# Memory output projection in one bank, token differences on DVE, weight stores on SP's queue

## The chip, the cores and the metric

One core of a Trainium2 chip runs the whole program in one launch. The metric is the device time of that launch in microseconds (us). TensorE (PE) does the matrix products; VectorE (DVE), ScalarE (ACT) and GpSimd (POOL) do element work; SyncE (SP) only issues DMA transfers, which ACT can issue too, each engine through a queue of its own.

## The reference, cut to what matters

One layer of a decoder on 2048 new prompt tokens and 32 sample tokens, width 1024, all in float32:

```python
def mem_attend(hn, mk, mv, wq_x, wo_x):
    q = (hn @ wq_x).reshape(B, T, MEM_HEADS, MEM_DH)
    s = jnp.einsum('bthd,bmhd->bhtm', q, mk) * (MEM_DH ** -0.5)
    p = jax.nn.softmax(s, axis=-1)
    o = jnp.einsum('bhtm,bmhd->bthd', p, mv).reshape(B, T, D_MODEL)
    return o @ wo_x

def conv_ffn(hn, buf, w_gate, w_up, conv_w, conv_b, w_down):
    g = hn @ w_gate
    gp = jnp.concatenate([buf, g], axis=1)
    c = conv_b + sum(conv_w[j] * gp[:, j:j + T] for j in range(CONV_W))
    return (jax.nn.gelu(c) * (hn @ w_up)) @ w_down, gp[:, -(CONV_W - 1):]

def layer(x, ...):
    m, S, sv = mixer(rmsnorm(x, g_mix), s0, mix_p)
    h = x + m
    h = h + mem_attend(rmsnorm(h, g_x), mk, mv, wq_x, wo_x)
    f, new_buf = conv_ffn(rmsnorm(h, g_ffn), buf, ...)
    return h + f, S, new_buf, sv
```

The FFN is 2816 wide, the memory has 256 tokens and 4 heads.

## The kernel before

The prompt runs in four blocks of 512 tokens; the sample tokens ride with block 1 in the mixer and with block 2 in the FFN, whose tiles are then 544 wide. Activations are kept transposed: h is eight tiles of 128 model rows by the block's tokens, and "m" numbers these tiles. Float32 accuracy comes from splitting every operand into a high part (ACT, L84) and a low part (DVE, L85); `mm3` (L91 to 94) then issues three matmuls for one product, high by high, high by low and low by high.

Each block goes through norm, input projection, gated linear attention and SGU, an output projection (tiles `wo`), memory attention, a memory output projection (tiles `wx`), and the FFN. Values and output weights of the memory are folded beforehand into `vod`, so the `wx` stage multiplies the softened and transposed probabilities (`pTh`, `pTl`, made by `turn` from p for each head, two k tiles a head) with `vod`. It is a product with 8 k tiles for each of the 8 m tiles. `out_proj_steps` writes it as steps `half(m2, k0, last)`: for the m tiles 2 m2 and 2 m2 + 1, four k tiles from k0 on, 12 matmuls of 512 columns into an accumulator bank, and a DVE add of the bank to h (L1167). The list x1 holds the four steps with k0 = 0, x2 those with k0 = 4. So every m tile takes two banks and two adds, and the m tiles are finished in x2, one after the other. In `finish(m)` ACT scales h (`wxg`, L1175) and squares it (`wxq`, L1187), and POOL sums the squares over m (`wxsq`, L1192).

Blocks 1 to 3 do the FFN's gate and up products with seven block products in place of eight (`seven_step`, gate rows `wg`, up rows `wup`). These need sums and differences of weights, and of tokens: `seven_tokens` takes two scaled m tiles and makes t13 on DVE (L188, L189), t24 on POOL (L190, L191), and the high and low parts of the four operands: `w` (A11), `wbh`/`wbl`, `wth`/`wtl` and `wuh`/`wul`. The first gate product of a block runs "early": it goes through the first three token pairs for all seven products (names such as `a_wg30A`, `a_wg30S`) and then takes the last pair, m = 6 and 7. Beside it `stat` multiplies the sum of squares with a column of ones (`wxss`, L1199), DVE makes `rt` (L300), POOL raises it to the power -1/2 (`wxrs`, L301), DVE writes it on a diagonal (`dg_f`, L308) and PE spreads it over partitions (`bcp_f`, L309).

Block 0 does its FFN with plain products from weights that it loads, 512 KB a unit, on SP's queue (L102). While they are here it also makes what blocks 1 to 3 will load: split weights (`wkeep` for the down projection, array wd) and, in `seven_make`, the plain parts (w7g, w7u) and the sums (s7g, s7u). Their stores, 2 for each down unit, 10 for a gate and 8 for an up unit, 440 in all, go through `put` and `flush` (L290 to 296): `put` lists a store, `flush` issues what is listed on ACT's queue, two steps later or when the next unit is made. The stores of the folded memory weights go the same way, earlier.

`run` makes weight units five ahead of the step that uses them. Pools set how far work runs ahead: 4 accumulator banks and 4 more banks in PSUM, 5 raw weight buffers, 5 each of high and low weights, 49 wide token tiles. The order on each engine is set by a scheduler of the tile framework from the program's order, the dependences and its own estimate of times. `weave` (near the end of the program) merges lists of steps: the scores of the four heads and x1 form one list, and the turns of the four heads are put in at places 1, 2, 3 and 5.

Of the kernel before, what the change touches and what calls it, by code (L numbers as in the profile page):

```python
# [37 lines left out]
def hymba_step_kernel(  # L38
# [9 lines left out]
    nc = tc.nc  # L48
# [80 lines left out]
    def wkeep(dst, *spec):  # L129

        def load():
            out = wunit(*spec)
            flush()
            for x, t in enumerate(out):
                put(dst[:, x], t.bitcast(F32))
            return out
        return load
# [16 lines left out]
    def seven_make(raw, hi, lo, plain, sums, u, name):  # L154
# [10 lines left out]
        ks = slice(2 * u, 2 * u + 2)  # L165
        flush()
        for x, t in enumerate((hi, lo)):
            t = t.bitcast(F32).rearrange("p (k two) m -> p two k m", two=2)
            for k in range(2):
                put(plain[:, k, x, ks], t[:, k, :, 0:128])  # L170
            put(plain[:, 2, x, ks], t[:, 1, :, 128:256])
        for i, t in enumerate((s13, s24)):
            d = sums[:, 2 * i:2 * i + 2]
            v = lambda t: t.rearrange("p (s k m) -> p s k m", s=2, k=2)
            if len(sums.shape) == 4:
                put(d[:, :, ks], v(t[:, :512]))
                continue
            sh, sl = U(f"sh{i}{name}", F32R), U(f"sl{i}{name}", F32R)
            split(sh[:, :512], sl[:, :512], t[:, :512])
            for x, o in enumerate((sh, sl)):  # L180
                put(d[:, :, x, ks], v(o[:, :512].bitcast(F32)))

    def seven_tokens(a, b, H, name):
# [5 lines left out]
        dve.tensor_tensor(t13[:, hi_], B22, B12, ALU.subtract)  # L189
        pool.tensor_tensor(t24[:, lo_], B22, t13[:, lo_], ALU.subtract)  # L190
        pool.tensor_tensor(t24[:, hi_], B21, t24[:, lo_], ALU.subtract)  # L191
        one = U(f"w1{name}", F32R)
# [950 lines left out]

    def out_proj_steps(B, unit, src, g, name, sample, first, finished, keep=None, seven=False):

# [5 lines left out]

        def half(m2, k0, last):
            def fn(wu):
                wh, wl = wu
                x = src()
                if m2 == 0 and last:
                    B.hn, B.sq = [], None
                for mm in range(2):
                    m = 2 * m2 + mm
                    ms = slice(mm * 128, (mm + 1) * 128)  # L1160
                    for ci, (c0, cw) in enumerate(chunks_of(sample)):
                        cs = slice(c0, c0 + cw)
                        ps = acc(f"a_{name}{s}{k0}{m}{ci}")
                        for k in range(4):
                            mm3(ps[:, :cw], wh[:, k, ms], wl[:, k, ms], x[k0 + k][0][:, cs], x[k0 + k][1][:, cs],
                                k == 0, k == 3)
                        dve.tensor_tensor(B.h[m][:, cs], ps[:, :cw], B.h[m][:, cs], ALU.add)  # L1167
                    if last:
                        finish(m)
# [34 lines left out]

        second = 4 - first
        return ([half(m2, first, False) for m2 in range(4)], [half(m2, second, True) for m2 in range(4)], Step(stat))


# [400 lines left out]
    for s, B in enumerate(blocks):  # L1609
# [5 lines left out]
        if B.mix_sample:  # L1615
            def keep():
                if not hasattr(smp, "x"):
# [7 lines left out]
        x1, x2, xstat = out_proj_steps(B, lambda k0, m2, s=s: wready(vod[m2][k0 // 4], f"wx{s}{k0}{m2}"),  # L1625
                                       lambda B=B: B.ao, "gffn", "wx", False, 0, B.ffn_sample, seven=s > 0)
        steps += w2 + [stat, scales]
        steps += weave(sc + x1, (turns[:1], 1, 1), (turns[1:2], 2, 2), (turns[2:3], 3, 3), (turns[3:], 5, 5))
        fin = final_steps(B)
# [48 lines left out]
```

## Time and profile before

| | us |
|---|---|
| median of three runs | 2936.9 |
| lowest, highest | 2928.57, 2940.09 |
| the profiled execution | 2934.86 |
| its span, first to last instruction | 2933.1 |
| TensorE busy in it | 2870.4 |
| VectorE busy | 1816.2 |
| ScalarE busy | 1048.8 |
| GpSimd busy | 697.4 |
| mean granted TensorE clock, as a share of full speed | 0.988 |

All rows of the trace come from the one profiled execution, whose time is its span and 1.8 us around it. Engines work beside each other, so busy times don't add up to the span. A waiting time says which instruction had to be done before the waiting one could start. The block ends that matter lie near 1176, 1888 and 2570 us (blocks 1, 2 and 3, from the memory output projection to the FFN), and block 0's FFN lies between 400 and 800 us.

### The profile page before, as it was taken

The numbers are of one execution on the slowest core, as the hardware profiler recorded it, in microseconds if no ns is written. First come the engines' busy times: TensorE is split into PE (matmuls) and PEld (weight loads), VectorE is DVE, ScalarE is ACT, GpSimd is POOL, SyncE is SP. The second block draws the span as 40 slices with busy tenths as digits, with TensorE's granted clock in tenths as the row PEclk, the third lists the DMA queues.
The fourth block names the chain that finished last, engine by engine and source line by source line (L and its number), as shares of the span: only waits on it lengthen the run. The fifth ranks groups of instructions, "written<-read, shape, count | busy, mean of one in ns | idle before, by whom it ended". The sixth has DMA issues, their size and how long they took to land.

```text
span 2933.1 us, 47340 instructions
## 1 busy us (share of the span) xinstructions
PE 2870.4 (98%) x18148; PEld 2533.2 (86%) x18148; DVE 1816.2 (62%) x3109; ACT 1048.8 (36%) x1904; POOL 697.4 (24%) x724
## 2 busy tenths in 40 slices
PE   8999999999999999999999999999999999999998
PEld 8887887887887898888888879899999788899998
DVE  6566567777746544645556674566666685475555
ACT  5635334333462423312223543422223534331222
POOL 1222112111122321312223231332222232141221
PEclk9999999999999999999999999999999999999999
DMA  9645679999832235776896214477776323567774
GB/s 309 198 144 184 204 231 324 344 343 337 301 104 64 67 115 184 277 277 246 306 327 232 84 58 151 167 254 262 252 266 223 105 67 106 182 245 253 281 278 179
DMA packets 360137, 625.48 MB, mean 213 GB/s; under 512 B 27195, under 2 KB 227838, under 8 KB 359912
## 3 DMA queue, kind: packets, MB, share of 16 engines
q1 hardware_dynamic: 232040, 513.37, 51.5%
q10 hardware_dynamic: 127872, 109.09, 11.0%
q8 instruction: 144, 2.36, 0.3%
q14 instruction: 81, 0.66, 0.1%
HBM read 497.04 MB, written 125.31 MB: 212 GB/s over the span
## 4 chain that ended last, share of the span: by engine, by line
PE 77%; DVE 6%; DMA 2%; ACT 2%; issue 1%; POOL 1%; ACTq 0%; DVEq 0%; POOLq 0%; SPq 0%
PE d L92 5%; PE d L94 5%; PE d L93 5%; PE sc L94 2%; PE sc L93 2%; PE sc L92 2%; PE a_wo L92 2%; PE a_wo L93 2%; PE a_wo L94 2%; PE a_wx L92 1%; PE a_wx L93 1%; PE a_wx L94 1%; PE a_wup L92 1%; PE a_wup L93 1%; PE a_wup L94 1%
## 5 line engine op out<-in xcount | busy, mean ns | idle before, releaser
L92 PE MATMUL d<-acth,whi_wd 128*128 128x512 f32 (+2 forms) x720 | 244.8, 340 | 0.0
L94 PE MATMUL d<-acth,wlo_wd 128*128 128x512 f32 (+2 forms) x720 | 243.2, 338 | 0.0
L93 PE MATMUL d<-actl,whi_wd 128*128 128x512 f32 (+2 forms) x720 | 242.7, 337 | 0.0
L1532 DVE TENSOR_TENSOR h<-d,h 128x512 f32<-128x512 f32 (+1 forms) x232 | 133.5, 583 | 159.4 <-PE d L94 159.2
L1471 POOL TENSOR_TENSOR c<-c,bc_f 128x512 f32<-128x512 f32 (+1 forms) x88 | 130.4, 1484 | 158.9 <-ACT c L1470 158.2
L94 PEld LDWEIGHTS d<-acth,wlo_wd 128*128 128x128 f32 x720 | 135.5, 188 | 16.0 <-issue 1.6
L92 PEld LDWEIGHTS d<-acth,whi_wd 128*128 128x128 f32 x720 | 135.5, 188 | 15.2 <-issue 1.6
L93 PEld LDWEIGHTS d<-actl,whi_wd 128*128 128x128 f32 x720 | 135.6, 188 | 14.4 <-issue 0.8
L94 PE MATMUL sc<-whi_qk,wol 128*128 128x256 f32 x512 | 144.5, 283 | 0.0
L92 PE MATMUL sc<-whi_qk,woh 128*128 128x256 f32 x512 | 144.3, 283 | 0.0
L93 PE MATMUL sc<-wlo_qk,woh 128*128 128x256 f32 x512 | 143.9, 282 | 0.0
L1461 ACT ACTIVATE c<-g,colsb 128x512 f32<-128x512 f32 x88 | 71.7, 814 | 200.8 <-DVE g L1430 142.6
L1493 POOL TENSOR_TENSOR c<-r_q_wup,c 128x512 f32<-128x512 f32 (+1 forms) x33 | 59.3, 1796 | 340.2 <-DVE r_q_wup L281 216.2
L1458 POOL COPY carry<-g 128x2 f32<-128x2 f32 x88 | 33.2, 377 | 423.1 <-DVE g L1430 421.0
L980 POOL TENSOR_TENSOR e<-e,k 128x512 f32<-128x512 f32 (+1 forms) x48 | 71.8, 1497 | 211.7 <-DVE kr L976 137.2
L92 PE MATMUL a_wo<-ch,h_wo 128*128 128x512 f32 (+1 forms) x320 | 113.2, 362 | 7.2 <-ACT ch L84 6.0
L93 PE MATMUL a_wo<-cl,h_wo 128*128 128x512 f32 (+1 forms) x320 | 113.9, 358 | 0.4 <-POOL cl L85 0.4
L94 PE MATMUL a_wo<-ch,l_wo 128*128 128x512 f32 (+1 forms) x320 | 113.3, 356 | 0.0
L1462 DVE SCALAR_TENSOR_TENSOR c<-g,colsb,c 128x512 f32<-128x512 f32 x88 | 86.9, 987 | 26.9 <-ACT c L1461 24.9
L92 PE MATMUL a_wx<-pTh,whi_wx 128*128 128x512 f32 x256 | 101.4, 396 | 0.0
L93 PE MATMUL a_wx<-pTl,whi_wx 128*128 128x512 f32 x256 | 100.6, 393 | 0.0
L94 PE MATMUL a_wx<-pTh,wlo_wx 128*128 128x512 f32 x256 | 100.6, 393 | 0.0
(3354 smaller groups left out, 9616.5 us busy)
## 6 DMA issues: line engine op xcount, KB each, us to landing
whi_wd<-wd SPq DMA_DIRECT2D x66, 512.0 KB
wlo_wd<-wd SPq DMA_DIRECT2D x66, 512.0 KB
r_wo<-in_w_out_dram SPq DMA_DIRECT2D x32, 512.0 KB
whi_qk<-qkd SPq DMA_DIRECT2D x32, 512.0 KB
wlo_qk<-qkd SPq DMA_DIRECT2D x32, 512.0 KB
wlo_wx<-vod SPq DMA_DIRECT2D x32, 512.0 KB
whi_wx<-vod SPq DMA_DIRECT2D x32, 512.0 KB
r_wg<-in_w_gate_dram SPq DMA_DIRECT2D x22, 512.0 KB
```

The source lines that it names most:

```text
L92: pe.matmul(ps, wh, xh, start=first, stop=False)
L93: pe.matmul(ps, wh, xl, start=False, stop=False)
L94: pe.matmul(ps, wl, xh, start=False, stop=last)
L980: pool.tensor_tensor(kl[:, :Tl], e[:, :Tl], B.k[p][:, :Tl], ALU.mult)
L1458: pool.tensor_copy(carry[:, f, :], g[:, SB:SB + 2])
L1461: act.activation(c[:, :SB], g[:, 2:SB + 2], AF.Identity, bias=cb, scale=w2)
L1462: dve.scalar_tensor_tensor(c[:, :SB], g[:, 1:SB + 1], w1, c[:, :SB], ALU.mult, ALU.add)
L1471: pool.tensor_tensor(c[:, :T], c[:, :T], B.fbc[:, :T], ALU.mult)
L1493: (dve, pool)[i].tensor_tensor(c[:, :T], q[i], c[:, :T], ALU.mult)
L1532: dve.tensor_tensor(B.h[m + mm][:, cs], ps[:, :cw], B.h[m + mm][:, cs], ALU.add)
```

## The change

It has three parts. (1) `out_proj_steps` gets a mode `whole`, used for `wx` in all four blocks. For m tiles 0 to 3 the first four k open a bank that stays open, in two steps, and two more steps close them; for m tiles 4 and 5, and then 6 and 7, a step with the first four k and a step with the last four follow each other. h is added once for each m tile, when its bank closes. The turn of head 3 moves from behind the second step of the stage to behind the first. (2) The two t24 differences move from POOL to DVE. (3) Block 0's 440 weight stores are issued on SP's queue, in the program right behind the unit that makes them, without the list. The stores of the folded memory weights stay on ACT.

```diff
         def load():
             out = wunit(*spec)
-            flush()
             for x, t in enumerate(out):
-                put(dst[:, x], t.bitcast(F32))
+                nc.sync.dma_start(dst[:, x], t.bitcast(F32))
...
-        flush()
         for x, t in enumerate((hi, lo)):
             t = t.bitcast(F32).rearrange("p (k two) m -> p two k m", two=2)
             for k in range(2):
-                put(plain[:, k, x, ks], t[:, k, :, 0:128])
-            put(plain[:, 2, x, ks], t[:, 1, :, 128:256])
+                nc.sync.dma_start(plain[:, k, x, ks], t[:, k, :, 0:128])
+            nc.sync.dma_start(plain[:, 2, x, ks], t[:, 1, :, 128:256])
...
-                put(d[:, :, ks], v(t[:, :512]))
+                nc.sync.dma_start(d[:, :, ks], v(t[:, :512]))
...
-                put(d[:, :, x, ks], v(o[:, :512].bitcast(F32)))
+                nc.sync.dma_start(d[:, :, x, ks], v(o[:, :512].bitcast(F32)))
...
-        pool.tensor_tensor(t24[:, lo_], B22, t13[:, lo_], ALU.subtract)
-        pool.tensor_tensor(t24[:, hi_], B21, t24[:, lo_], ALU.subtract)
+        dve.tensor_tensor(t24[:, lo_], B22, t13[:, lo_], ALU.subtract)
+        dve.tensor_tensor(t24[:, hi_], B21, t24[:, lo_], ALU.subtract)
...
-        def half(m2, k0, last):
+        open_ = {}
+
+        def half(m2, k0, last, begin=True, end=True):
...
-                        ps = acc(f"a_{name}{s}{k0}{m}{ci}")
+                        ps = acc(f"a_{name}{s}{k0}{m}{ci}") if begin else open_.pop(m)
                         for k in range(4):
                             mm3(ps[:, :cw], wh[:, k, ms], wl[:, k, ms], x[k0 + k][0][:, cs], x[k0 + k][1][:, cs],
-                                k == 0, k == 3)
-                        dve.tensor_tensor(B.h[m][:, cs], ps[:, :cw], B.h[m][:, cs], ALU.add)
+                                begin and k == 0, end and k == 3)
+                        if end:
+                            dve.tensor_tensor(B.h[m][:, cs], ps[:, :cw], B.h[m][:, cs], ALU.add)
+                        else:
+                            open_[m] = ps
...
         second = 4 - first
+        if whole:
+            out = [half(m2, first, False, end=False) for m2 in (0, 1)]
+            out += [half(m2, second, True, begin=False) for m2 in (0, 1)]
+            for m2 in (2, 3):
+                out += [half(m2, first, False, end=False), half(m2, second, True, begin=False)]
+            return out[:2], out[2:], Step(stat)
...
-        steps += weave(sc + x1, (turns[:1], 1, 1), (turns[1:2], 2, 2), (turns[2:3], 3, 3), (turns[3:], 5, 5))
+        steps += weave(sc + x1, (turns[:1], 1, 1), (turns[1:2], 2, 2), (turns[2:3], 3, 3), (turns[3:], 4, 4))
```

On DVE at the end of block 3's `wx` stage this stood before; h_6 and h_7 are the adds of the last two m tiles, `wtl_25663` and `wul_25667` belong to the pair before, `l_wup30S` is the low part of a weight.

```order
L1167 TENSOR_TENSOR h3_6_22821<-a_wx3460_25679,h3_6_22821 128x512
L85 TENSOR_TENSOR wtl35_25663<-t1335_25649,wth35_25662 128x512
L85 TENSOR_TENSOR wul35_25667<-t2435_25650,wuh35_25666 128x512
L1167 TENSOR_TENSOR h3_7_22822<-a_wx3470_25698,h3_7_22822 128x512
L85 TENSOR_TENSOR w137_25720<-wxg36_25693,w137_25720 128x256
L188 TENSOR_TENSOR t1337_25714<-wxg36_25693 128x256
L85 TENSOR_TENSOR l_wup30S2_25676<-r_wup30S2_25673,h_wup30S2_25675 128x1024
L189 TENSOR_TENSOR t1337_25714<-wxg37_25712,wxg36_25693 128x256
L85 TENSOR_TENSOR wbl37_25724<-wxg37_25712,wbh37_25723 128x512
L85 TENSOR_TENSOR wtl37_25728<-t1337_25714,wth37_25727 128x512
L85 TENSOR_TENSOR wul37_25732<-t2437_25715,wuh37_25731 128x512
```

And this stands there now:

```order
L1171 TENSOR_TENSOR h3_6_22773<-a_wx3060_25585,h3_6_22773 128x512
L85 TENSOR_TENSOR w137_25656<-wxg36_25630,w137_25656 128x256
L1171 TENSOR_TENSOR h3_7_22774<-a_wx3070_25598,h3_7_22774 128x512
L186 TENSOR_TENSOR t1337_25650<-wxg36_25630 128x256
L85 TENSOR_TENSOR l_wup30S2_25614<-r_wup30S2_25611,h_wup30S2_25613 128x1024
L187 TENSOR_TENSOR t1337_25650<-wxg37_25648,wxg36_25630 128x256
L188 TENSOR_TENSOR t2437_25651<-wxg37_25648,t1337_25650 128x256
L85 TENSOR_TENSOR wbl37_25660<-wxg37_25648,wbh37_25659 128x512
L189 TENSOR_TENSOR t2437_25651<-wxg37_25648,t2437_25651 128x256
L85 TENSOR_TENSOR wtl37_25664<-t1337_25650,wth37_25663 128x512
L85 TENSOR_TENSOR wul37_25668<-t2437_25651,wuh37_25667 128x512
```

One add for each tile is left, the pair before no longer stands between the last adds, and the two t24 differences (L188 and L189 of the new numbering) have come in ahead of `wbl` and ahead of `wtl`.

On PE at the same place, the end of the early part of the first gate product, before; `w_`, `wb`, `wt` and `wu` numbered 257xx are the operands of the last pair:

```order
L92 MATMUL a_wg30A12_25799<-wbh37_25723,wg30A12_25483 128x256
L93 MATMUL a_wg30A12_25799<-wbl37_25724,wg30A12_25483 128x256
L94 MATMUL a_wg30A12_25799<-wbh37_25723,wg30A12_25483 128x256
L92 MATMUL a_wg30S1_25789<-wth37_25727,wg30S1_25453 128x256
L92 MATMUL a_wg30S2_25809<-wuh37_25731,wg30S2_25485 128x256
L93 MATMUL a_wg30S1_25789<-wtl37_25728,wg30S1_25453 128x256
L94 MATMUL a_wg30S1_25789<-wth37_25727,wg30S1_25453 128x256
L1199 MATMUL wxss3_25738<-ones_86,wxsq3_25505 128x1 x4
L92 MATMUL a_wup30A11_25915<-w131_25529,wup30A11_25612 128x256
```

And now:

```order
L92 MATMUL a_wg30A12_25735<-wbh37_25659,wg30A12_25490 128x256
L92 MATMUL a_wg30S1_25725<-wth37_25663,wg30S1_25431 128x256
L93 MATMUL a_wg30A12_25735<-wbl37_25660,wg30A12_25490 128x256
L94 MATMUL a_wg30A12_25735<-wbh37_25659,wg30A12_25490 128x256
L1205 MATMUL wxss3_25674<-ones_86,wxsq3_25388 128x1 x4
L93 MATMUL a_wg30S1_25725<-wtl37_25664,wg30S1_25431 128x256
L94 MATMUL a_wg30S1_25725<-wth37_25663,wg30S1_25431 128x256
L92 MATMUL a_wg30S2_25745<-wuh37_25667,wg30S2_25492 128x256
L92 MATMUL a_wup30A11_25851<-w131_25411,wup30A11_25583 128x256
```

The statistic `wxss` has moved ahead of the product with `wtl`.

On SP in the middle of block 0's FFN only loads stood before:

```order
L102 DMA r_wg020_4770<-in_w_gate_dram 128x4x256
L102 DMA r_wg021_4858<-in_w_gate_dram 128x4x256
L102 DMA r_wd000_4888<-in_w_down_dram 128x4x256
L102 DMA r_wd002_4974<-in_w_down_dram 128x4x256
L102 DMA r_wd004_4982<-in_w_down_dram 128x4x256
```

Now stores (w7g and w7u from the high and low weights, s7g from the sums) stand between the loads:

```order
L168 DMA w7u0_183<-l_wup001_4485 128x2x128 x2
L169 DMA w7u0_183<-l_wup001_4485 128x2x128
L179 DMA s7g1_186<-sh0wg010_4546 128x2x256
L179 DMA s7g1_186<-sl0wg010_4547 128x2x256
L179 DMA s7g1_186<-sh1wg010_4552 128x2x256
L179 DMA s7g1_186<-sl1wg010_4553 128x2x256
L102 DMA r_wg020_4762<-in_w_gate_dram 128x4x256
L168 DMA w7g1_185<-h_wg010_4530 128x2x128 x2
L169 DMA w7g1_185<-h_wg010_4530 128x2x128
L168 DMA w7g1_185<-l_wg010_4531 128x2x128 x2
L169 DMA w7g1_185<-l_wg010_4531 128x2x128
L102 DMA r_wg021_4852<-in_w_gate_dram 128x4x256
```

A load now follows up to ten stores on SP's queue.

## Rows read from the trace of the kernel before

**Rows 1.** Page part 1: busy us, share of span, instructions.

```profile
PE 2870.4 (98%) x18148; PEld 2533.2 (86%) x18148; DVE 1816.2 (62%) x3109; ACT 1048.8 (36%) x1904; POOL 697.4 (24%) x724
```

**Rows 2.** Waits of PE, whole run: total us, times, longest.

```profile
PE a_wg30A L93 <- DVE wbl L85: 2.1, 1, 2.1
...
PE a_wg30S L93 <- DVE wtl L85: 1.0, 1, 1.0
```

**Rows 3.** Windows of PE: length, busy (matmuls), granted clock, DMA share, GB/s.

```profile
1175.50:1193.00 17.50, 14.82 (x99) 0.80 0.27 87
1887.00:1908.00 21.00, 17.34 (x114) 0.84 0.30 101
2569.20:2587.00 17.80, 14.71 (x95) 0.81 0.28 93
2578.40:2585.20 6.80, 6.75 (x31) 0.50 0.40 125
2600.00:2617.80 17.80, 17.80 (x154) 1.00 0.87 293
1960.00:1981.00 21.00, 21.00 (x171) 1.00 0.55 182
```

**Rows 4.** Timeline of DVE, block 3: start, length, line, work, idle before.

```profile
2571.16 0.68 DVE L1167 TENSOR_TENSOR h<-a_wx,h 128x512 f32<-128x512 f32 x1
...
2572.60 0.41 DVE L188 TENSOR_TENSOR t<-wxg 128x256 f32<-128x256 f32 x1
2572.93 1.21 DVE L85 TENSOR_TENSOR l_wup30S<-r_wup30S,h_wup30S 128x1024 fp32r<-128x1024 f32 x1
...
2574.93 1.21 DVE L85 TENSOR_TENSOR wbl<-wxg,wbh 128x512 fp32r<-128x512 f32 x1
2576.06 1.77 DVE L85 TENSOR_TENSOR wtl<-t,wth 128x512 fp32r<-128x512 f32 x1
```

**Rows 5.** Timeline of PE, the same place.

```profile
2569.22 0.28 PE L92 MATMUL a_wg30A<-w,wg30A 128*128 128x256 f32 x1
...
2576.20 0.39 PE L93 MATMUL a_wg30A<-wbl,wg30A 128*128 128x256 f32 x1 [2.09 <-DVE wbl L85]
...
2578.23 1.53 PE L1199 MATMUL wxss<-ones,wxsq 128*128 128x1 f32 x8
...
2583.38 0.63 PE L309 MATMUL bcp_f<-dg_f,ones 128*128 128x128 f32 x2
```

**Rows 6.** Timeline of ACT, the same place.

```profile
2571.89 0.71 ACT L1175 ACTIVATE wxg<-h,colsb 128x512 f32<-128x512 f32 x1
2572.64 0.63 ACT L84 ACTIVATE wbh<-wxg 128x512 fp32r<-128x512 f32 x1
```

**Rows 7.** Timeline of POOL, the same place.

```profile
2573.15 1.57 POOL L190 TENSOR_TENSOR t<-wxg,t 128x256 f32<-128x256 f32 x1 [0.76 <-DVE t L188]
...
2575.55 1.73 POOL L1192 TENSOR_TENSOR wxsq<-wxsq,wxq 128x512 f32<-128x512 f32 x1
2580.04 2.03 POOL L301 TENSOR_TENSOR wxrs<-rt,neghalf 128x4 f32<-128x4 f32 x1 [2.76 <-DVE rt L300]
```

**Rows 8.** Windows of PE: block 0's FFN, its middle, and after the stores.

```profile
400.00:800.00 400.00, 396.58 (x1729) 1.00 1.00 325
600.00:650.00 50.00, 49.93 (x218) 1.00 1.04 344
1500.00:1550.00 50.00, 50.00 (x450) 1.00 0.97 359
```

**Rows 9.** Issues of one kind of store on ACT: ns min/median/max.

```profile
L296 ACTq DMA_DIRECT2D w7g<-h_wg x66: 366/508/1961, 409.2 to 745.5; - x66
```

**Rows 10.** Timeline of all engines: a load's issue and its split.

```profile
759.53 0.37 SPq L102 DMA_DIRECT2D r_wd<-in_w_down_dram  x1
...
776.06 1.06 ACT L84 ACTIVATE h_wd<-r_wd 128x1024 fp32r<-128x1024 f32 x1 [1.27 <-DVE l_wd L85]
```

**Rows 11.** Timeline of DVE: softened probabilities of head 3, block 3.

```profile
2525.93 0.62 DVE L1252 TENSOR_SCALAR p<-p,mx 128x256 f32<-128x256 f32 x2
```

More of the change, by code (lines that the diff above doesn't have):

```diff
@@ L1141, in gla_steps, with out_proj_steps @@
         return [Step(f) for f in out], [Step(f) for f in tail]
-    def out_proj_steps(B, unit, src, g, name, sample, first, finished, keep=None, seven=False):
+    def out_proj_steps(B, unit, src, g, name, sample, first, finished, keep=None, seven=False,
+                       whole=False):
         s = B.s
@@ L1625, in hymba_step_kernel @@
         x1, x2, xstat = out_proj_steps(B, lambda k0, m2, s=s: wready(vod[m2][k0 // 4], f"wx{s}{k0}{m2}"),
-                                       lambda B=B: B.ao, "gffn", "wx", False, 0, B.ffn_sample, seven=s > 0)
+                                       lambda B=B: B.ao, "gffn", "wx", False, 0, B.ffn_sample, seven=s > 0, whole=True)
         steps += w2 + [stat, scales]
-        steps += weave(sc + x1, (turns[:1], 1, 1), (turns[1:2], 2, 2), (turns[2:3], 3, 3), (turns[3:], 5, 5))
+        steps += weave(sc + x1, (turns[:1], 1, 1), (turns[1:2], 2, 2), (turns[2:3], 3, 3), (turns[3:], 4, 4))
         fin = final_steps(B)
```

## The prediction, made before the changed kernel was run

> **What bounds the kernel now.** I read the page's head first. TensorE (PE) is busy 98% of the span, DVE 62%, ACT 36%, POOL 24% [rows 1]. On average PE is the bound, and nothing in the change takes a matmul from it, so a gain can only come out of the 2% in which it idles and out of stretches at its lower clock. I then asked for PE's waits, and kept those that the change can touch. In each of blocks 1 to 3 the first gate product of the FFN waits about 2 us for `wbl`, DVE's low half of the last token pair, and then about 1 us for `wtl` of the same pair; the rows of block 3 stand for three such pairs [rows 2]. The stretch around each was then laid beside one of equal length with a full PE [rows 3]. The full stretch has 154 matmuls in 17.8 us, 0.1156 us each; where sample tokens ride (block 2) it is 171 in 21 us, 0.1228 each. The block ends have 99 in 17.5 us (151 would fit), 114 in 21 and 95 in 17.8. Short by 52, 57 and 59 matmuls, they lose 6.0 + 7.0 + 6.8 = **19.8 us**. Only 3 us of each is the waiting: behind the two waits the granted clock stands at 0.50, the 1.2 GHz level, for 6.8 us (block 3's row stands for the three [rows 3]), and PE does half of its work there, 3.4 us more.
>
> Why is `wbl` late? PE leaves the last `a_wx` tile at T = 2569.22, but DVE adds it into h only at 2571.16 [rows 4, 5]: it is behind with the pair before. A tile's four k are 12 matmuls of 0.229 us (50 us / 218 [rows 8]), 2.75 us, so pairs of m tiles follow each other every 5.5 us, and a pair's splits, differences and adds fill that on DVE. The last pair then needs scale on ACT, differences, hi and lo, one behind the other.
>
> **The change part by part.** *One bank, one add.* Before, all eight m tiles close in the second half of the stage, 2.75 us apart. Now the eight k of m = 4 to 7 run in pairs of tiles, 48 matmuls, so a pair comes every 11 us. PE's matmuls stay the same, and 32 DVE adds of 0.68 us go (22 us of DVE, off the path). What counts is the last pair: DVE has emptied its queue by T. The chain from T, with durations of before [rows 4, 6]: add of h at T+0.4 (0.4 is my estimate for the way from PE to an idle DVE), done T+1.1; scale on ACT 0.71, T+1.85; `wbh` 0.63, T+2.5. On DVE meanwhile `l_wup30S` 1.21 is queued ahead of what waits for ACT (order of after), done T+2.3; the second t13 and the first t24 0.41 each (DVE's price for such a difference, by the t row [rows 4]), T+3.1; `wbl` 1.2, **T+4.3**. PE asks for it at T+4.9, the time at which its wait began before (2576.20 - 2.09 [rows 5]). So this wait goes, with 0.6 us to spare. `wtl`: second t24 0.41 and `wtl` between 0.68, as the add of the same size, and 1.77 [rows 4], T+5.4 to T+6.5, asked for at T+6.0, since `wxss` now stands ahead of it. Mostly gone. The sum that feeds `wxss`: squares on ACT done near T+3.1, POOL's add 1.73 [rows 7], T+4.8, asked for at T+5.1. Gone, barely.
>
> *Differences on DVE.* On POOL the first of the last pair took 1.57 us from 2573.15 on, and the sum, behind both, started at 2575.55 [rows 7]. On DVE they cost 2 x 0.41 for each pair, 24 x 0.41 = 10 us in all, in an engine just relieved of 22, and POOL's sum starts as soon as its squares are there. The moved work is hidden by the 11 us that a pair now has; without that cover it would put 0.8 us per block on the path.
>
> *What is late next.* After `wxss` comes the chain rt, the power on POOL (2.03 us [rows 7]), the diagonal on DVE, and PE's `bcp_f`. Before, `bcp_f` stood 2583.38 - 2579.76 = 3.6 us behind the end of `wxss` [rows 5], filled with 15 matmuls at half clock. By the order of after there are 17; at full clock 17 x 0.1156 = 2.0 us pass, and the chain needs 0.16 + 2.03 + 0.22 + the handoffs, 2.65 to 3.4. PE will wait here 0.65 to 1.45 us where it did not wait before. I take 1.3, nearer the upper end, since each handoff in these rows adds a tenth or two. Over three blocks that gives 3.9 us back: 19.8 - 3.9 = **15.9 us gained** if the clock then stays up.
>
> *Turn of head 3.* It moves two tiles' halves earlier; 168 of the stage's 192 matmuls, 38.5 us, and its own eight transposes come behind it, so PE reaches it near T - 39.5 = 2529.7. It needs the softened p of 2525.93 + 0.62 [rows 11]: 3 us of cover. Its user now comes 5.5 us behind it, against the 1.3 us that hi and lo take. Cost nothing; without the cover, up to 3 us a block.
>
> *Block 0's stores on SP.* 440 DMA issues leave ACT for SP's queue, right among the loads. What it can gain is bounded by what PE loses in block 0's FFN, 400 - 396.6 = 3.4 us [rows 8]; its few waits are on DVE (h and g), which ACT feeds. I take 1, bounds 0 to 3.4. What it can cost: one gate, up and down triple is 3 units of 24 matmuls, 16.5 us of PE, and 20 stores and 3 loads on SP. A load's issue takes 0.37 us there [rows 10]; a store's median on ACT is 0.51 for the kind shown, single ones up to 1.96 [rows 9]. At 0.51 SP needs 20 x 0.51 + 1.1 = 11.3 of 16.5 us: not the bound. A load that has to stand behind a unit's ten stores comes 10 x 0.51 = 5.1 us later, and the shortest time from a load's issue to its split is 16.5 us (759.53 to 776.06 [rows 10]), some of it the transfer itself; so 5 us are covered, and 12 would not be. The DMA engines are full in this stretch either way (share 1.04, 344 GB/s [rows 8]), and near 1500, with the stores over and SP alone issuing, it was 359 GB/s [rows 8], so the bandwidth stays.
>
> Here the Trainium skill speaks against the edit. "DMA: Bandwidth & Descriptors", section "Queues, rings and completion order", says that each DMA engine alternates between the queues that have work and takes the descriptors of one queue in order. By that a load, which had a turn of its own beside ACT's stores, would now wait for all bytes queued ahead of it. This case's rows of before cannot show it, since no store stands ahead of a load there. A gate unit's ten stores are 1.84 MB by their shapes, at 344 GB/s an estimated 5.3 us per load, which the 16.5 us take up once but not if two units' stores gather; the sum above would stay, and the rival D below is where it would show.
>
> Sum: 2934.9 (the profiled execution; 2933.1 of it span) - 15.9 - 1 = **2918 us**. That execution lies 2 us under the median of the three runs, 2936.9; I leave that as noise.
>
> **The rivals.** A, the forecast, 2918; its bounds are 1.45 against 0.65 us at `bcp_f` (2 us), 0 to 3.4 in block 0, and `wtl` late by up to 0.5 a block: 2914 to 2921.
>
> B, a new wait takes the place of the old. PE stands 1.3 us at `bcp_f` right behind the eight one-column matmuls of `wxss`, and the clock falls again. For it: before, it fell behind 2 + 1 us of waiting. Against it: 1.3 us is less. Each block then gives back the 3.4 us: 2918 + 10 = 2928.
>
> C, DVE stays the bound of the last pair. `l_wup30S` goes first, and `wtl` takes 1.77 us beside POOL's sum against 0.68 for the add of the same size [rows 4, 7]; the sum stays on POOL. If `wbl` is 1 us late in each block and the clock falls in half of them, half of the gain is left: 2926.
>
> D, slower: SP becomes the bound of block 0's FFN. The point is 20 s + 1.1 = 16.5, a mean of s = 0.77 us per store. At 0.85 the triple takes 18.1 us, 1.6 x 22 = 35 us lost: 2918 + 35 = 2953. For it: ACT's longest issues (1.96), loads and stores on one full queue, and in-order waiting of SP for splits. Against it: the median of 0.51.
>
> E, better: no wait at `bcp_f` and all of block 0's 3.4 us: 2934.9 - 19.8 - 3.4 = 2912.
>
> That the change does not do what it says is ruled out by the order of the new kernel: adds, differences and stores stand where the diff says.
>
> **How the numbers follow.** Half a per cent of 2936.9, 14.7 us, is about what a measurement of this kernel can tell from no change; faster means under 2922. A 0.55, B 0.20, C 0.10, D 0.07, E 0.08. The likeliest gives 2918. The range goes from under E by the runs' own scatter to over B by as much, 2909 to 2933, and leaves D out with a little of the rest. A and E are faster, less the part of A that lies above 2922, and B's and C's small part below: 0.58; B, C and that part of A within: 0.35; D slower: 0.07.
>
> **What would show it.** PE's waits for `wbl` and `wtl` gone from all three blocks, h's last add within 0.5 us of T, and the clock of the 17.5 us windows near 1.00: part one right. A row of PE waiting for `dg_f`, about 1 us, is foreseen; with 0.50 behind it, B. POOL's sum starting at T+3 confirms the differences. In block 0, SP's issues near 0.5 us and PE's idle time no larger than 3.4 us; PE waiting there for `h_wg` or `l_wg` behind late loads means D. The prediction is wrong if the windows keep 0.8, or if block 0's FFN grows by more than 5 us.

## The result, and the profile after

The changed kernel takes 2916.6 us in the median (2911.8 to 2922.0, 6 runs) against 2931.7 before in the same comparison: a ratio of 0.9944, 95% interval 0.9925 to 0.9963. In a second comparison it took 2916.8 us, ratio 0.9938, interval 0.9925 to 0.9951. So it is faster by 0.6%; the medians differ by 15 us in the first comparison and by 18 in the second. The forecast was 2918, range 2909 to 2933.

Head of the page of the changed kernel: its span, then busy time, share and instructions of each engine.

```profile
span 2910.1 us, 47402 instructions
...
PE 2854.9 (98%) x18148; PEld 2524.1 (87%) x18148; DVE 1795.9 (62%) x3101; ACT 1049.8 (36%) x1904; POOL 672.1 (23%) x700
```

The span is 23 us shorter than that of before; the profiled execution is the fastest of its six. DVE is busy for 20 us less [rows 1]. 22 us of adds are gone and 18 of differences have come (24 of them, 0.75 us in the mean, since some stretch beside POOL's sums); but the low parts of the token pairs on DVE take 12 us less now that POOL makes no differences beside them. POOL is busy for 25 us less.

These are the three block ends in windows of the same length as before, from PE's leaving the last `a_wx` tile (window, PE busy and matmuls, granted clock, DMA share, GB/s).

```profile
1170.70:1188.20 17.50, 16.94 (x142) 1.00 0.53 168
1876.10:1897.10 21.00, 19.98 (x157) 1.00 0.40 128
2551.30:2569.10 17.80, 17.26 (x144) 1.00 0.51 167
```

Against [rows 3]: 142, 157 and 144 matmuls in place of 99, 114 and 95, and a granted clock of 1.00 in all three.

To lay stages of several kernels side by side, the table gives the time between the same two matmuls of PE's order in each trace (the statistic's matmuls left out of the count). Block 0's FFN is counted from within its `wx` stage (400 us in the kernel before). A block end runs from within the `wx` stage to behind `bcp_f`, 215 to 236 matmuls; "mixer" is block 1 from the end of block 0's FFN to its attention.

| profile of | block 0's FFN | mixer, block 1 | end, block 1 | end, block 2 | end, block 3 |
|---|---|---|---|---|---|
| before | 400.2 | 299.9 | 39.83 | 49.92 | 40.07 |
| before, second profile | 400.7 | 297.0 | 38.87 | 50.08 | 39.92 |
| changed | 395.1 | 303.3 | 34.57 | 44.49 | 34.36 |
| changed, second profile | 395.1 | 297.8 | 34.57 | 45.79 | 34.33 |
| single add alone | 400.8 | 309.6 | 35.93 | 46.11 | 36.94 |
| differences alone | 401.3 | 305.3 | 35.31 | 49.29 | 38.96 |
| stores alone | 396.2 | 299.9 | 39.84 | 49.97 | 40.11 |
| single add and differences | 401.4 | 306.0 | 34.61 | 45.79 | 34.35 |
| stores on SP, by the list | 396.2 | 303.5 | 39.97 | 49.72 | 40.08 |
| stores direct on ACT | 408.4 | 302.2 | 40.10 | 49.87 | 40.02 |
| stores in halves | 558.7 | 297.8 | 34.66 | 44.49 | 34.26 |
| statistic from two sums | 395.1 | 303.0 | 34.39 | 43.89 | 34.20 |

The changed kernel gains 5.3 + 5.4 + 5.7 = 16.4 us at the block ends and 5.1 in block 0's FFN, in its first profile. The stage of block 1's attention, in which one of the moved turns lies, takes 60.1 before and 60.0 after.

What PE still waits for at the block ends (all three together; total, times, longest):

```profile
PE a_wg20S L93 <- DVE wtl L85: 1.0, 1, 1.0
...
PE wxss L1205 <- POOL wxsq L1198: 1.0, 2, 0.5
```

The waits for `wbl` [rows 2] are gone. That for `wtl` is left in block 2, and blocks 1 and 3 have a new one of 0.5 us, for POOL's sum of squares. The end of block 3 shows both sides, first on DVE (start, length, line, work).

```profile
2551.10 1.39 DVE L85 TENSOR_TENSOR w<-wxg,w 128x256 fp32r<-128x256 f32 x1 [1.68 <-ACT w L84]
2552.41 0.68 DVE L1171 TENSOR_TENSOR h<-a_wx,h 128x512 f32<-128x512 f32 x1
...
2555.15 0.68 DVE L85 TENSOR_TENSOR wbl<-wxg,wbh 128x512 fp32r<-128x512 f32 x1
2555.75 1.49 DVE L189 TENSOR_TENSOR t<-wxg,t 128x256 f32<-128x256 f32 x1
2557.16 0.68 DVE L85 TENSOR_TENSOR wtl<-t,wth 128x512 fp32r<-128x512 f32 x1
```

POOL at the same place, and then PE:

```profile
2550.90 1.30 POOL L1198 TENSOR_TENSOR wxsq<-wxsq,wxq 128x512 f32<-128x512 f32 x1 [5.39 <-ACT wxq L1193]
2555.17 1.79 POOL L1198 TENSOR_TENSOR wxsq<-wxsq,wxq 128x512 f32<-128x512 f32 x1 [2.97 <-ACT wxq L1193]
2558.78 1.02 POOL L299 TENSOR_TENSOR wxrs<-rt,neghalf 128x4 f32<-128x4 f32 x1 [1.82 <-DVE rt L298]
```

```profile
2551.31 0.27 PE L92 MATMUL a_wg30A<-w,wg30A 128*128 128x256 f32 x1
...
2557.01 1.05 PE L1205 MATMUL wxss<-ones,wxsq 128*128 128x1 f32 x8 [0.47 <-POOL wxsq L1198]
...
2559.92 0.28 PE L94 MATMUL a_wg30S<-wuh,wg30S 128*128 128x256 f32 x1
2560.27 0.46 PE L307 MATMUL bcp_f<-dg_f,ones 128*128 128x128 f32 x2
```

PE leaves its last `a_wx` tile at T = 2551.31. The add of it comes at T+1.1, against T+1.9 before [rows 4, 5]: DVE is not behind any more, but the low part `w`, which stands ahead, takes 1.39 us beside POOL's sum for the tile before (2550.90 to 2552.20). `wbl` is done at 2555.83, T+4.5, 0.3 us before PE asks. POOL's last sum runs from 2555.17 to 2556.96; the second t24 difference (L189), begun beside it at 2555.75, takes 1.49 us, though its like takes 0.41 [rows 4]. PE waits 0.47 us for that sum at `wxss`, and comes to `bcp_f` 0.35 us behind the matmul ahead of it, where 0.12 is its pace: the power on POOL took 1.02 us and not 2.03 [rows 7].

### The profile page after: what moved, and what is told of

The parts are those of the page before. It is cut to its first block, busy times and chain, and to the rows that moved or that the text cites. A ratio compares the mean times of both kernels' runs of the same rounds, so it can differ in the third digit from the quotient of the medians.

```text
span 2910.1 us, 47402 instructions
## 1 busy us (share of the span) xinstructions
PE 2854.9 (98%) x18148; PEld 2524.1 (87%) x18148; DVE 1795.9 (62%) x3101; ACT 1049.8 (36%) x1904; POOL 672.1 (23%) x700
## 4 chain that ended last, share of the span: by engine, by line
PE 83%; DVE 3%; issue 1%; DMA 1%; ACT 1%; POOL 1%; DVEq 0%; POOLq 0%; SPq 0%; ACTq 0%
PE d L94 6%; PE d L92 6%; PE d L93 6%; PE sc L94 2%; PE sc L93 2%; PE sc L92 2%; PE a_wx L94 2%; PE a_wx L92 2%; PE a_wx L93 2%; PE a_wo L92 2%; PE a_wo L93 2%; PE a_wo L94 2%; PE a_wg L92 1%; PE a_wup L92 1%; PE a_wup L93 1%; PE a_wg L93 1%
## 5 line engine op out<-in xcount | busy, mean ns | idle before, releaser
L92 PEld LDWEIGHTS d<-acth,whi_wd 128*128 128x128 f32 x720 | 135.4, 188 | 15.1 <-issue 1.6
```

What stands on the lines that cost most here:

```text
L92: pe.matmul(ps, wh, xh, start=first, stop=False)
```

## Each part alone, and two of them together

The theory behind these four: the block ends gain from DVE being free when PE leaves the last tile, and from POOL being free for the sum; block 0 gains from ACT being free of store issues. The rivals put the whole gain on one part.

**Single add alone.** The edit is the changed kernel with the two differences back on POOL and the stores back in the list:

```diff
-        dve.tensor_tensor(t24[:, lo_], B22, t13[:, lo_], ALU.subtract)
-        dve.tensor_tensor(t24[:, hi_], B21, t24[:, lo_], ALU.subtract)
+        pool.tensor_tensor(t24[:, lo_], B22, t13[:, lo_], ALU.subtract)
+        pool.tensor_tensor(t24[:, hi_], B21, t24[:, lo_], ALU.subtract)
...
-                nc.sync.dma_start(dst[:, x], t.bitcast(F32))
+                put(dst[:, x], t.bitcast(F32))
```

> One bank and one add for each m tile of wx, with the turn moved; differences stay on POOL, stores on ACT's queue. Theory (the block ends gain from DVE being free at T and, for the sum, from POOL being free of the differences): DVE's add of the last tile within 0.5 us of PE's leaving it and no wait for wbl, but POOL takes 1.57 + 0.79 us for the differences before its sum, so PE waits 1.5 to 2.5 us for wuh or for the sum; half of the 15.8 us, 8 us, is gained, 2924. Rival 1 (the single add alone does it): all of 15.8, 2916. Rival 2 (the differences alone do it): 0 to 3 us, 2929 to 2932, with the waits for wbl and wtl as before.

Measured: 2931.0 us, ratio 0.9984 (0.9971 to 0.9997). In its profile the block ends gain 3.9 + 3.8 + 3.1 = 10.8 us. DVE's rows at the end of block 3: the last add, which comes 1.0 us behind PE's last `a_wx` tile, and the weight's low part behind the statistic.

```profile
2572.44 0.68 DVE L1173 TENSOR_TENSOR h<-a_wx,h 128x512 f32<-128x512 f32 x1
...
2579.98 1.23 DVE L85 TENSOR_TENSOR l_wup30S<-r_wup30S,h_wup30S 128x1024 fp32r<-128x1024 f32 x1
```

PE's waits there:

```profile
PE a_wg30S L93 <- DVE wtl L85: 0.9, 1, 0.9
PE a_wg30A L93 <- DVE wbl L85: 0.4, 1, 0.4
```

At the block ends the theory's direction held, its detail did not: PE waits for `wbl` (0.4) and `wtl` (0.9), not for `wuh` or the sum. In the median the kernel gains only 2.2 us, 0.9 to 8.5 by the interval, which is the time of Rival 2, though the waits are not as before; this profile loses 9.7 us in block 1's mixer, and whether the other executions do is not shown. By the stages, neither the single add nor the differences carry everything. The single add also halves DVE's adds and doubles the time between pairs at once, and no run parts these two.

**Differences alone.** The kernel before with

```diff
-        pool.tensor_tensor(t24[:, lo_], B22, t13[:, lo_], ALU.subtract)
-        pool.tensor_tensor(t24[:, hi_], B21, t24[:, lo_], ALU.subtract)
+        dve.tensor_tensor(t24[:, lo_], B22, t13[:, lo_], ALU.subtract)
+        dve.tensor_tensor(t24[:, hi_], B21, t24[:, lo_], ALU.subtract)
```

> Only the two t24 differences on DVE. Theory: DVE, which is behind already with 6.6 us of work for a pair that comes every 5.5, gets 0.8 us more for each pair; its last add comes later than 2 us behind T, the waits for wbl stay near 2 us or grow, the clock falls in all three blocks: no gain, 2930 to 2936. Rival 1: the same, 2932. Rival 2 (the differences do it): the waits go, 2916 to 2920.

Measured: 2928.7 us, ratio 0.9982 (0.9970 to 0.9993): a small gain where I had expected none. The three block ends in windows, then PE's waits at them:

```profile
1179.40:1196.90 17.50, 16.43 (x137) 1.00 0.34 122
1885.60:1906.60 21.00, 18.31 (x118) 0.84 0.25 90
2564.30:2582.10 17.80, 15.88 (x103) 0.81 0.33 118
```

```profile
PE a_wg30S L92 <- ACT wth L84: 1.6, 1, 1.6
...
PE a_wg20S L92 <- ACT wth L84: 1.4, 1, 1.4
...
PE a_wg10S L92 <- ACT wth L84: 1.1, 1, 1.1
...
PE a_wg20A L93 <- DVE wbl L85: 1.0, 1, 1.0
```

`wbl` is waited for in block 2 alone, but `wth` has come in its place, 1.1 to 1.6 us in each block. Block 1 has the one wait of 1.1 us, keeps its clock at 1.00 and gains 4.5 us; block 2, with 1.4 and 1.0 us and a small one, falls to the lower clock and gains 0.6; block 3, with 1.6 and another 0.4, falls too and gains 1.1. DVE's last add came 0.2 us behind PE's last `a_wx` tile in block 1, 2.8 in block 2 and 0.8 in block 3. So the differences on POOL had a share in the lateness that my sum did not give them. On DVE the 24 differences take 15.0 us, but the low parts of the token pairs (`w`, `wbl`, `wtl`, `wul`) take 37.6 us in place of 52.4, so DVE has no more to do than before, and the waits get shorter.

**Stores alone.** The kernel before with the stores as in the change.

> Only block 0's 440 stores on SP's queue. Theory (ACT's long store issues held back splits, DVE waited for them and freed PE's banks late): block 0's FFN loses its four stalls of PE, 5 us gained, 2927, block ends of 1 to 3 unchanged with 99, 114 and 95 matmuls in their windows. Rival (the gain in block 0 came with the single adds of its wx stage, which free 5.5 us of DVE): the stalls near 500 us stay, 2932. Rival D of the prediction (SP the bound): slower, 2945 or more.

Measured: 2930.7 us, ratio 0.9990 (0.9977 to 1.0002). By time it can't be told from no change, but the trace can tell: block 0's FFN and the end of block 1 in windows.

```profile
397.00:792.00 395.00, 395.00 (x1718) 1.00 1.02 330
1169.60:1187.10 17.50, 14.66 (x98) 0.80 0.28 85
```

PE is busy through all of block 0's FFN (396.2 us against 400.2), and the block end is as before (98 matmuls, clock 0.80).

**Single add and differences, stores on ACT.**

> The changed kernel with the stores back on ACT's queue and the list. Theory: all of the block ends' 15.8 us and nothing in block 0, 2916 + 5 = 2921, with PE's stalls near 500 and 707 us back. Rival (the stores cost elsewhere what they gain in block 0, in the step from block 0 to 1): the same time as the changed kernel or less, 2912 to 2917.

Measured: 2923.4 us, ratio 0.9969 (0.9957 to 0.9980). The block ends gain 5.22 + 4.13 + 5.72 = 15.1 us, block 0's FFN nothing (401.4 us). The two parts therefore divide as forecast, in the stages; the median gains 9.8 us. That the stores cost elsewhere what they gain is refuted: with them the kernel is faster (2916.8 us, and the two intervals do not overlap), and in their own profile the block ends and the mixer are as before.

## What held PE up in block 0

The forecast gave the stores 1 us, and named ACT's issues only as a possible feeder of the waits. In the kernel before, ACT's rows around 500 us are

```profile
500.54 2.75 ACTq L296 DMA_DIRECT2D w7u<-l_wup  x2
503.33 1.06 ACT L84 ACTIVATE h_wup<-r_wup 128x1024 fp32r<-128x1024 f32 x1 [3.10 <-DVE s24wg L163]
```

and DVE's behind them

```profile
504.43 1.23 DVE L85 TENSOR_TENSOR l_wup<-r_wup,h_wup 128x1024 fp32r<-128x1024 f32 x1 [1.14 <-ACT h_wup L84]
505.57 0.69 DVE L1532 TENSOR_TENSOR h<-d,h 128x512 f32<-128x512 f32 x1
```

Two stores keep ACT for 2.75 us, but most of that is not issuing. The second of them starts only at

```profile
502.92 0.37 ACTq L296 DMA_DIRECT2D w7u<-l_wup  x1
```

and between the two ACT's queue waits for 1.8 us, by the profile for an earlier store. The high part `h_wup` starts only then (`s24wg`, which its label names, is not among its operands); DVE waits for it before `l_wup`, and the add of h, which frees PE's bank, stands behind that and ends a stall of PE at 506.40. PE has five stalls in this stage, which end near 497, 503, 506, 513 and 709 us and make up 3.4 us. ACT waits for stores in many places of the stage, 107 us in all by the profile; the largest such row is

```profile
ACT sh0wg L84 <- DMA w7g<-h_wg: 22.2, 5, 5.3
```

and no row of this kind has more than 1.2 us in the changed kernel. Whether the issues or the waits between them weigh more was not tried. Three kernels, with the stores' own above, part the queue from the list that delays the stores.

**Stores on SP, through the list as before:**

```diff
-    def put(dst, src):
-        late.append((now[0], dst, src))
+    def put(dst, src, eng=nc.scalar):
+        late.append((now[0], eng, dst, src))
...
-            nc.scalar.dma_start(dst, src)
+            eng.dma_start(dst, src)
...
-                put(dst[:, x], t.bitcast(F32))
+                put(dst[:, x], t.bitcast(F32), nc.sync)
```

> The kernel before with block 0's stores on SP's queue, but through the list of put and flush, one unit or two steps late as before. Theory (what held PE up in block 0 was ACT's time in the issues): block 0's FFN as with the direct stores, 395 to 397 us against 400 before. Rival (the list's lateness held buffers and so the splits): 399 to 401 us as before. If SP then waits less for splits, nothing more is to be had, since PE is already without a stall there.

Measured: 2933.5 us, ratio 0.9992 (0.9982 to 1.0002), and in the window of block 0's FFN

```profile
400.00:800.00 400.00, 400.00 (x1750) 1.00 1.01 328
```

no idle time: the queue does it, not the list.

**Stores directly on ACT**, the change with `nc.scalar` for `nc.sync`:

> The kernel before with block 0's stores still on ACT's queue, but issued directly behind their unit, without the list. Theory (ACT's time in the issues holds PE up): stalls stay, block 0's FFN 400 us or more, since ACT now also waits in order for DVE's halves: 400 to 406. Rival (the list's lateness did it): 395 to 397 us.

Measured: 2944.9 us, ratio 1.0024 (1.0009 to 1.0038). PE's waits for DVE's add of h, and DVE's rows at one of them:

```profile
PE d L92 <- DVE h L1530: 6.3, 2, 3.4
```

```profile
571.05 1.46 DVE L85 TENSOR_TENSOR l_wup<-r_wup,h_wup 128x1024 fp32r<-128x1024 f32 x1 [4.44 <-ACT h_wup L84]
...
573.04 1.27 DVE L1530 TENSOR_TENSOR h<-d,h 128x512 f32<-128x512 f32 x2
```

DVE waits 4.4 us for ACT's `h_wup`. Block 0's FFN takes 408.4 us, beyond the 406 that the theory allowed. The list was a good remedy for ACT's queue, and on SP's it is not needed.

**Stores in halves**, for the slower case that the prediction named (SP as the bound): the changed kernel with each store issued as two, 880 in all.

```diff
-                nc.sync.dma_start(plain[:, k, x, ks], t[:, k, :, 0:128])
+                for y in range(2):
+                    nc.sync.dma_start(plain[:, k, x, 2 * u + y], t[:, k, y, 0:128])
```

> The changed kernel with each of the 440 stores on SP issued as two halves, 880 issues and the same bytes. Rival D of the prediction (SP becomes the bound when 20 stores and 3 loads of a triple take more than PE's 16.5 us): 40 x 0.5 + 3 x 0.5 = 21.5 us a triple, block 0's FFN grows by 5 x 22 = 110 us to about 505 us, 3025 us in all. If a half costs only the 0.36 us that is the shortest issue, 16 us a triple: at the edge, 395 to 405 us. Other theory (the issue time on SP is not a cost of the issue but back-pressure of full DMA engines, so half a store takes half of it): no growth, 395 us.

Measured: 3076.3 us, ratio 1.0484 (1.0465 to 1.0502). The issue of one kind of store in the changed kernel (ns, min/median/max), and then in halves:

```profile
L168 SPq DMA_DIRECT2D w7g<-h_wg x44: 359/511/1702, 408.5 to 744.2; - x44
```

```profile
L172 SPq DMA_DIRECT2D w7g<-h_wg x88: 320/430/500, 407.8 to 898.8; - x88
```

A half costs 0.43 us, not half of 0.51. Over all kinds the 880 stores take 0.44 us in the mean and the 440 took 0.61, so the price is mostly for the issue, and the issues of twice as many stores keep SP for 386 us in place of 268. Block 0's FFN in one window, and PE's waits in it:

```profile
397.00:955.70 558.70, 413.00 (x1730) 0.86 0.73 231
```

```profile
PE d L92 <- ACT h_wd L84: 57.7, 4, 21.8
PE a_wg L92 <- ACT h_wg L84: 46.6, 3, 24.3
PE a_wup L92 <- ACT h_wup L84: 37.9, 2, 21.8
```

PE waits up to 24 us for high parts of weights that were loaded late, at a DMA share of 0.73. So the danger was real and its place was right. 40 x 0.43 + 3 x 0.5 = 18.7 us a triple would make 48 us over PE's 16.5; measured are 164. PE is idle for 146 of them, and its matmuls, at a mean clock of 0.86, take 18 us longer (413.0 us, 394.9 in the changed kernel). The issues of the window add up to 431 us of SP's time, more than the 395 that PE needs; what the idle time holds beyond that is not accounted for, and SP's in-order waits for splits are only a likely cause. How near the changed kernel comes to the edge: its 511 issues on SP between 397 and 790 us, added up from their rows, take 316 us of 393, 80%. The prediction had 11.3 of 16.5 us, 68%.

## The waits that are left

**The changed kernel again**, for its interval and a second profile.

> The changed kernel once more, for a narrower interval and a second profile. Theory (the stages give 16.4 us at the block ends and 5.1 in block 0; what the medians show beside that is the clock of block 1's mixer, which moves from run to run): block ends of 34 to 35, 44 to 45 and 34 us and block 0's FFN of 395 us again, block 1's mixer anywhere from 300 to 310 us, 2914 to 2920 in the median. Rival (the change costs something in block 1's mixer): that stage 3 us or more above the 299.9 of before again, ratio above 0.9955.

Measured: 2916.8 us, ratio 0.9938 (0.9925 to 0.9951). Block ends and block 0 repeat, but for block 2; block 1's mixer, expected at 300 to 310 us, took 297.8.

```profile
1874.90:1895.90 21.00, 19.98 (x146) 0.92 0.33 111
```

This is block 2's window. It has the same 1.0 us wait for `wtl` as in the first profile, and this time the clock falls for part of the window: 146 matmuls against 157, 1.3 us.

**The kernel before again.**

> The kernel before once more, for a second profile of it. Theory (block 1's mixer moves with the clock from run to run, whatever the kernel): block ends of 40, 50 and 40 us and block 0's FFN of 400 us again with PE's four stalls near 500 and 707 us, block 1's mixer somewhere between 297 and 310 us. Rival (the changed order lengthens that mixer): 299.9 us again, within 0.5.

Measured: 2933.9 us, ratio 0.9993 (0.9980 to 1.0007). The mixer of block 1 took 297.0 us here and 299.9 in the first profile; in the changed kernel 303.3 and 297.8. Over twelve profiles of kernels with either order it lies between 297 and 310, so the 3.4 us that the first pair of profiles seemed to lose there lies within the scatter. Block 0's FFN takes 400.7 us again, but PE's stalls, five again, lie elsewhere: near 502, 511, 573, 640 and 708 us, 3.9 us in all.

**Statistic from two sums.** The changed kernel, with PE adding the last tile's squares itself in place of POOL's last add:

```diff
+            if seven and m == 7:
+                B.sq7 = t
-            if m == 0:
+            elif m == 0:
...
-                pe.matmul(ps[:n, c:c + 1], B.sq[:, c * 128:c * 128 + n], ones[:, 0:1], start=True, stop=True)
+                pe.matmul(ps[:n, c:c + 1], B.sq[:, c * 128:c * 128 + n], ones[:, 0:1], start=True, stop=not seven)
+                if seven:
+                    pe.matmul(ps[:n, c:c + 1], B.sq7[:, c * 128:c * 128 + n], ones[:, 0:1], start=False, stop=True)
```

> The changed kernel without POOL's last add of squares in blocks 1 to 3: PE adds the squares of the last tile to the statistic itself, with four more one-column matmuls. Theory (POOL's 1.79 us are what PE waits for at wxss, and they stand beside DVE's second difference, which takes 1.49 instead of 0.41 us): PE's waits of 0.5 us at wxss and of 1.0 us for wtl in block 2 go, DVE's difference takes 0.41 us, each block end is 0.5 to 1.2 us shorter, 2 to 3 us in all, not to be told from the changed kernel in the median (2913 to 2918). Rival (the matmul order or the new tile's buffer costs as much): block ends as in the changed kernel or longer.

Measured: 2913.8 us, ratio 0.9931 (0.9919 to 0.9942). POOL at the end of block 3, and DVE's second difference:

```profile
2551.32 1.30 POOL L1200 TENSOR_TENSOR wxsq<-wxsq,wxq 128x512 f32<-128x512 f32 x1 [5.37 <-ACT wxq L1193]
2558.56 1.02 POOL L299 TENSOR_TENSOR wxrs<-rt,neghalf 128x4 f32<-128x4 f32 x1 [5.94 <-DVE rt L298]
```

```profile
2556.17 0.41 DVE L189 TENSOR_TENSOR t<-wxg,t 128x256 f32<-128x256 f32 x1
```

Between its sum of the tile before, at 2551.32, and the power POOL has nothing to do, and the difference takes 0.41 us. At the block ends PE waits for neither `wtl` nor a sum. The ends are 0.2, 0.6 and 0.2 us shorter than the changed kernel's in its first profile (in block 2, 1.3 + 0.6 = 1.9 than in its second), mostly less than the 0.5 to 1.2 expected; the added one-column matmuls, eight a block (ten in block 2) at the pace of 0.12 us, cost about 1 us of it by that estimate. It has the lowest median of the kernels run and is faster than before; from the changed kernel the times can't tell it, as expected.

## Why the prediction was right

*The loss at the block ends* was 19.8 us by counting matmuls, and 15.9 of it were to come back. By the same count 9, 14 and 10 matmuls are still missing, 1.0 + 1.7 + 1.2 = 3.9 us, so 15.9 came back; between like matmuls it is 16.4 in one profile and 15.1 in the other. The sum was right to a fraction of a microsecond, and partly for other reasons than mine.

*Single add: DVE free, the last add at T+0.4.* It came at T+1.1. The step failed by 0.7 us, since I had left out that POOL's sum of the tile before stretches DVE's `w`: 1.39 us in these rows, 0.41 where it runs alone. `wbl` was forecast for T+4.3 and came at T+4.5, because it took 0.68 us and not 1.2; PE asked at T+4.8. No wait, as forecast.

*`wtl`: T+5.4 to T+6.5 against T+6.0, "mostly gone".* T+6.5. Gone in blocks 1 and 3, where the late `wxss` hides it, 1.0 us left in block 2, where tiles are 544 wide.

*The sum: T+4.8 against T+5.1, "barely".* It came at T+5.65, late by what the add was late, and PE waited 0.5 us for it in blocks 1 and 3. The step failed with the first one.

*The new wait at `bcp_f`, 1.3 us, bounds 0.65 to 1.45.* This step failed outright: 0.2 us. I had taken 2.03 us for the power from [rows 7]; it took 1.02. The rows of the single experiments say when. In the stores' kernel, where the end of block 3 is as before, DVE starts the low part of a weight

```profile
2574.83 1.23 DVE L85 TENSOR_TENSOR l_wup30S<-r_wup30S,h_wup30S 128x1024 fp32r<-128x1024 f32 x1
```

and POOL the power 0.06 us behind it:

```profile
2574.89 2.04 POOL L299 TENSOR_TENSOR wxrs<-rt,neghalf 128x4 f32<-128x4 f32 x1 [3.03 <-DVE rt L298]
```

In the single add's kernel the power starts first (2579.91, against 2579.98 for the same DVE work, shown above):

```profile
2579.91 1.02 POOL L301 TENSOR_TENSOR wxrs<-rt,neghalf 128x4 f32<-128x4 f32 x1 [2.17 <-DVE rt L300]
```

With DVE 0.06 us ahead it takes 2.04, with POOL 0.07 us ahead 1.02. The kernel before shows both: in block 1 of its second profile POOL comes first, 0.06 us ahead,

```profile
1182.37 1.02 POOL L301 TENSOR_TENSOR wxrs<-rt,neghalf 128x4 f32<-128x4 f32 x1 [2.18 <-DVE rt L300]
```

and that block end takes 38.87 us in place of 39.83. In the twelve profiles, 16 of the 36 powers of blocks 1 to 3 have DVE's low part 0.06 to 0.07 us ahead of them and take 2.03 or 2.04; the other 20, eight of them with that low part as little behind, take 1.02. In the changed kernel the low part comes behind the diagonal in blocks 1 and 3 (in block 3 at 2560.62) and 0.07 us behind the power in block 2. The Trainium skill states such a rule in "SBUF — State Buffer", section "Who interferes with whom": DVE with two inputs from SBUF and a GpSimd operation that reads SBUF exclude each other, and whichever comes second waits for the whole of the first. By that rule the power of before contained a wait of about 1 us, and the 16 rows agree, as do the 1.39 us of `w` and the 1.49 us of the difference beside POOL's sums; but DVE's low part took 1.22 or 1.23 us even where it came second to a power, so there the trace shows no wait.

The 1.1 us a block that I had too much here, 3.3 in all, stand against waits of 0.5, 1.0 and 0.5 us at the sum and at `wtl` that I had left out. So the 3.9 us still missing are the 3.9 of the forecast in size, not in place, and that is luck. PE is idle for only 2.1 of them in the three windows; the rest lies in matmuls that start behind their pace.

*Rival B, the clock falling again,* has a share: in block 2 the `wtl` wait let it fall for 1.3 us in the second profile of the changed kernel and in that of single add and differences, and not in the first or in the one with halves. Its place was another than the `bcp_f` that I had named. *Rival C* (DVE stays the bound) fell: no wait for `wbl`, and for `wtl` in block 2 alone.

*Differences: "hidden", and no gain of their own.* Underrated. They were charged with 24 x 0.41 = 10 us on DVE and credited with an earlier sum; they take 18.0 in the changed kernel, and alone they gain 6.3 us at the block ends. What the sum left out is that POOL's differences had stretched DVE's low parts: alone, the differences bring 15.0 us to DVE and take 14.8 off these (in the mean `wbl` falls from 1.16 to 0.88 us, `wul` from 1.40 to 0.85). What the shorter way from t13 to `wul` on one engine and the other order of DVE's rows do beside that was not tried.

*Block 0: 1 us, bounds 0 to 3.4.* Measured 5.1, of which the stores alone bring 4.0, and outside the bounds. The other 1.1 us are spread thinly over the stage, with no stall of PE in either kernel, and their cause is open. The term was mis-sized by its source: the busy share of the window [rows 8] counts PE as busy where it is not at its pace. The same 1729 matmuls that take 400 us before take 394.9 after:

```profile
397.10:792.00 394.90, 394.90 (x1729) 1.00 1.02 330
```

*Rival D: SP the bound of block 0.* Not reached, but shown to be there when issues double. That the DMA engines were less busy there (0.73) than in the changed kernel (1.02) points to SP's issuing rather than to the bytes queued ahead of a load; it does not show it. The first step of D is there in the changed kernel too: ACT and DVE wait for loads of weights in block 0, as in

```profile
ACT h_wd L84 <- DMA r_wd<-in_w_down_dram: 18.0, 5, 5.4
```

and in neither profile of the kernel before do they. A load's issue on SP takes 0.50 us in the median there, 0.37 before. The loads come later, and the units made ahead take it up: PE waits for no weight in block 0. What of the lateness is SP's issuing and what the order within one queue, no run here shows.

*Sum.* 16.4 + 5.1 = 21.5 us in the stages, 15 to 18 in the medians with an interval of 14 to 22 for the better measured one. The prediction's 17 lies within both; the stages say that it was low in block 0 by 4, and the medians carry the scatter of the mixers. In every kernel with a part of the change the median gains less than these stages do, by up to 8 us (single add alone), so it may not be scatter alone; that stays open.

## What to carry to other kernels

Price what PE loses at a stall by counting its matmuls against a full window of the same kind: the waits listed are only half of it where the clock falls behind them, and busy time is no bound on the gain. If a chain of small steps ends a stage, ask first whether the engine that starts it is still behind with the pair before; here spacing the pairs and halving their adds, which no run parts, gained more than the rest. Look also at what runs beside a small step on the other engine: moving a difference off POOL shortened DVE's own work by as much as it added. A DMA issue kept its engine for about half a microsecond, and halving its bytes took off less than a third, so put stores on an engine that computes nothing, and count issues there before splitting them.

## What the runs showed of the hardware

The order of two starts 0.06 us apart decided whether a 4-column power on POOL took 1.02 or 2.04 us, without exception in 24 cases; DVE's 1024-column subtraction took 1.22 or 1.23 us either way. A store of half the bytes kept SP for 0.43 us in place of 0.51. The same 1.0 us wait of PE was followed by the lower clock in one execution and not in another.
